# Sums of the output weights' quarters: from VectorE subtractions to DRAM copies and accumulating transfers

## The chip, the cores and the metric

The kernel runs on one core of a Trainium2 chip. The metric is the time of one execution in device microseconds. The engines are named as in the profile: PE (TensorE), PEld (its weight loads), DVE (VectorE), ACT (ScalarE), POOL (GpSimd) and SP (SyncE, which here only issues transfers). Sixteen DMA engines move the data.

## The reference

One encoder block with fp32 inputs: 1,024 tokens, width 2,048. A normalised input is projected to 5,632 columns; these feed windowed attention (16 heads, 4 key/value heads) and a bidirectional retention (8 heads); both branches are normalised and gated, put side by side and mixed by an output projection; residual and a final norm follow.

```python
h = rmsnorm(x, norm_w[l])
proj = jnp.einsum('bsd,de->bse', h, w_in[l])            # 1024 x 2048 x 5632
q_a, k_a, v_a, g_a, q_r, k_r, v_r, g_r = jnp.split(proj, points, axis=-1)
attn = rmsnorm(windowed_attention(q_a, k_a, v_a, ...), attn_out_norm_w[l]) * jax.nn.silu(g_a)
ret = head_groupnorm(bidirectional_retention(rotary(q_r), rotary(k_r) * 64**-0.5, v_r, ...), ret_gn_w[l]) * jax.nn.silu(g_r)
mixed = jnp.concatenate([attn, ret], axis=-1)
x = x + jnp.einsum('bse,ed->bsd', mixed, w_out[l])      # 1024 x 2048 x 2048
return rmsnorm(x, final_norm_w)
```

## The kernel before

**Arithmetic.** Every fp32 operand of the two projections is split into a rounded high part and the rest (`split`, L119 on): ACT casts the high part (`wh<-wr`, L127) and POOL or DVE subtracts it (`wl<-wr,wh`, L121). PE then makes three products per block: high by high, high by low, low by high.

**Input projection.** The weights come as 176 tiles of 128 x 512, called here by number from 0; 22 units (`UNITS`) of eight tiles each. `w_load` (L170) has SP load a tile into `wr` (two buffers), `w_split` (L175) makes `wh` and `wl` (two buffers each) of it. In the main loop (L919 on) each tile covers two steps of k; in the first of the two steps tile i + 1 is split and tile i + 2 loaded. The load's buffer is that of tile i, so SP waits until POOL has made `wl` of tile i. The buffers of `wh` and `wl` of tile i + 2 are free when PE has finished tile i.

**Work beside it.** After each quarter of a step `point` (L244) takes steps from three queues of generators: `jobs` (attention and retention), `aux` (evacuations, gates, the rotary step) and `slow` (bias rows, sums of weights, weighing and combining of rows). `slow` is served at two of three points, and at every point in the greater part of the output projection. The framework then orders each engine's instructions itself, so that work without dependences can stand well ahead of the place where it was issued.

**Output projection.** It works by a seven-product scheme on quarters, for each half f of the mixed width and each half u of the output columns: `quarter(f, u, j, q)` is the j-th tile of quarter q of the weights (q mod 2 is the column half, q // 2 the row half). Four of the seven products need a sum of quarters. These sums are made during the input projection by `w_combine` (L187): for each of the 16 (f, u, j) it loads the quarters into the two buffers `wc`, subtracts on DVE (L121), stores each sum into the DRAM tensor `wd`, and loads one of them again. A tile takes five loads, four subtractions and four stores. `w_src` (L163) later loads products 2 to 5 from `wd`. The same is done for the rows: `weigh_rows` scales the attention rows and `combine_rows` makes four combinations per (f, j) into the DRAM tensor `cd`, with three steps of `slow` between the loads and the DVE step. `done_with` (near the end) adds each finished product block into the output block e.

**Other parts the change touches.** `rope_post` loads the rotary tables just ahead of their use; in `attn_job` the gate of a block is loaded two steps ahead of the POOL multiplication that uses it.

Of the kernel before, what the change touches and what calls it, by code (L numbers as in the profile page):

```python
# [43 lines left out]
def hybrid_block(ctx: ExitStack, tc: tile.TileContext, a: dict, out: bass.AP):  # L44
# [57 lines left out]
    def wc_():  # L102
        return com.tile([128, 512], F32, tag="wc", name=nm("wc"), bufs=2)
# [82 lines left out]

    def w_combine(f):  # L187

        for u in range(2):
            for j in range(4):  # L190
                x, y = wc_(), wc_()
                SP.dma_start(x, quarter(f, u, j, 1))
                SP.dma_start(y, quarter(f, u, j, 0))
                yield from pause(3)
                tt(V, y, x, y, ALU.subtract)
                yield
                SP.dma_start(wd[f, u, 1, j], y)
                yield from pause(2)
                z = wc_()
                SP.dma_start(z, quarter(f, u, j, 3))  # L200
                yield from pause(3)
                tt(V, x, z, x, ALU.subtract)
                yield
                SP.dma_start(wd[f, u, 2, j], x)
                yield from pause(2)
                y = wc_()
                SP.dma_start(y, wd[f, u, 1, j])
                yield from pause(3)
                tt(V, z, z, y, ALU.subtract)
                yield  # L210
                SP.dma_start(wd[f, u, 0, j], z)
                v = wc_()
                SP.dma_start(v, quarter(f, u, j, 2))
                yield from pause(3)
                tt(V, v, v, z, ALU.subtract)
                yield
                SP.dma_start(wd[f, u, 3, j], v)
                yield from pause(2)

    def pause(n):  # L220
        for _ in range(n):
            yield
# [206 lines left out]
    def gate_post(tiles, et0, key):  # L429
# [7 lines left out]
        done.add(key)  # L437

    def rope_post(p, tiles, rq, rk):
        for hf in range(2):  # L440
            cs, sn = (retp[0].tile([128, 512], F32, tag="mr", name=nm("cs"), bufs=2) for _ in range(2))
            SP.dma_start(cs, a["cos"][:, 512 * hf : 512 * hf + 512])
            SP.dma_start(sn, a["sin"][:, 512 * hf : 512 * hf + 512])
            yield
            for et, dst in ((0, rq), (1, rk)):
                t = tiles[2 * et + hf]
                sh = retp[0].tile([128, 512], F32, tag="so", name=nm("sh"), bufs=2)
                V.stream_shuffle(sh, t, [i ^ 1 for i in range(32)])
                tt(V, t, t, cs, ALU.mult)
                yield  # L450
                tt(V, sh, sh, sn, ALU.mult)
                tt(V, dst[:, 512 * hf : 512 * hf + 512], t, sh, ALU.add)
                yield
        done.add(("rope", p))
# [4 lines left out]
    def attn_job(g, q_tiles, start):  # L459
# [36 lines left out]
        for t in range(32 + 8):  # L496
# [59 lines left out]
            if t >= 4 and t - 4 < 32:  # L556
# [220 lines left out]
    def weigh_rows():  # L777

        for hf in range(2):
            sl = slice(512 * hf, 512 * hf + 512)  # L780
            for kk in range(8):
# [3 lines left out]
                SP.dma_start(r, row)  # L785
                yield from pause(3)
                stt(V, r, r, ew[:, kk : kk + 1], n, ALU.mult, ALU.mult)
# [4 lines left out]
    def combine_rows(f, j, tile):  # L792

        if f:
            yield lambda: ("ret", j) in done
        for n, (x0, x1, op) in enumerate((
            (q_mix(f, j, 2), q_mix(f, j, 3), ALU.add),
            (q_mix(f, j, 0), q_mix(f, j, 2), ALU.subtract),
            (cd[f, 1, j], q_mix(f, j, 0), ALU.subtract),
            (q_mix(f, j, 1), cd[f, 0, j], ALU.subtract),  # L800
        )):
            x, y = tile(), tile()
            SP.dma_start(x, x0)
            SP.dma_start(y, x1)
            yield from pause(3)
            tt(V, y, x, y, op)
            yield
# [114 lines left out]
    for u, (kind, i) in enumerate(UNITS):  # L922
# [3 lines left out]
        for k in range(NK):  # L926
            step[0] = 16 * u + k
            wi, kk = divmod(step[0], 2)
            if kk == 0:
                w_split(wi + 1)  # L930
                w_load(wi + 2)
            if u == 0:
# [5 lines left out]
            for b in range(4):  # L938
# [16 lines left out]
                if last:  # L955
# [4 lines left out]
                    evac(u, b, p, st)  # L960
                point()
            if kind == "vr" and k == 9:
                if i == 0:
# [4 lines left out]
                else:  # L968
                    drain(jobs, ("ret", i - 1))
                raw = rope_t[i]  # L970
                rope_t[i] = (t4(), t4())
# [145 lines left out]
    for n in range(nprod):  # L1117
# [44 lines left out]
        def done_with(t):  # L1162
# [147 lines left out]
```

## Time and profile before

| what | value |
|---|---|
| median of three runs | 1634.11 us (1631.43 to 1637.33) |
| the profiled execution | 1634.68 us, its span 1632.9 us |
| mean TensorE clock granted | 0.976 of full |
| PE, PEld busy | 1530.8 us (94%), 1303.9 us (80%) |
| DVE, ACT, POOL busy | 890.5 us, 594.5 us, 467.3 us |
| moved by DMA | 261.49 MB, 160 GB/s in the mean |

The input projection takes the first 1,280 us or so, with attention beside it from about 200 us to 840 us and retention to 1,300 us; the output projection fills the rest. In a row of a timeline stand the start, the length (both in us), the engine, the line, the operation, out<-in, the shapes, and in brackets the idle time of the engine just before and what ended it. In a row of waits stand engine, line and tile that waited, what it waited for, and then the total in us, the number of times and the longest.

### The profile page before, as it was taken

The numbers are of one execution on the slowest core, as the hardware profiler recorded it, in microseconds if no ns is written. First come the engines' busy times: TensorE is split into PE (matmuls) and PEld (weight loads), VectorE is DVE, ScalarE is ACT, GpSimd is POOL, SyncE is SP. The second block draws the span as 40 slices with busy tenths as digits, with TensorE's granted clock in tenths as the row PEclk, the third lists the DMA queues.
The fourth block names the chain that finished last, engine by engine and source line by source line (L and its number), as shares of the span: only waits on it lengthen the run. The fifth ranks groups of instructions, "written<-read, shape, count | busy, mean of one in ns | idle before, by whom it ended". The sixth has DMA issues, their size and how long they took to land. (4 is left out here: it accounts for less than half of the span.)

```text
span 1632.9 us, 23154 instructions
## 1 busy us (share of the span) xinstructions
PE 1530.8 (94%) x8146; PEld 1303.9 (80%) x8146; DVE 890.5 (55%) x2000; ACT 594.5 (36%) x1254; POOL 467.3 (29%) x475
## 2 busy tenths in 40 slices
PE   8989998999999999999989989989989899899994
PEld 6977886778777887888988877888888777788883
DVE  5432265645665577566455655664647633537645
ACT  5321146543756367467411010110114322324434
POOL 2222222332343333334432221331323344420001
PEclk9999999999999999999999999999999999999998
DMA  8685545465445322312154554553255478666446
GB/s 294 244 240 170 174 150 163 163 196 163 152 148 178 106 62 72 84 57 79 49 162 149 171 190 149 181 187 101 82 180 168 136 235 274 213 217 195 124 122 226
DMA packets 163218, 261.49 MB, mean 160 GB/s; under 512 B 27371, under 2 KB 48875, under 8 KB 162972
## 3 DMA queue, kind: packets, MB, share of 16 engines
q1 hardware_dynamic: 163100, 259.99, 50.6%
q8 instruction: 64, 1.05, 0.3%
q14 instruction: 54, 0.44, 0.1%
HBM read 192.26 MB, written 67.67 MB: 159 GB/s over the span
## 5 line engine op out<-in xcount | busy, mean ns | idle before, releaser
L121 POOL TENSOR_TENSOR wl<-wr,wh 128x512 fp32r<-128x512 f32 x232 | 314.3, 1356 | 709.3 <-ACT wh L127 687.4
L127 ACT CAST wh<-wr 128x512 fp32r<-128x512 f32 x288 | 178.3, 619 | 608.0 <-PE psM L953 246.8
L121 DVE TENSOR_TENSOR wc<-wc,wc 128x512 f32<-128x512 f32 x92 | 79.5, 864 | 223.3 <-DMA wc<-in_w_out 98.2
L512 DVE CUSTOM_DVE_ANT_0 P<-psS,bias,nsink 128x384 f32<-128x384 f32 (+1 forms) x128 | 74.1, 579 | 60.5 <-PE psS L506 54.0
L516 ACT ACTIVATE P<-P,nmx 128x384 f32<-128x384 f32 (+1 forms) x128 | 75.6, 591 | 83.5 <-DVE nmx L512 82.3
L121 POOL TENSOR_TENSOR acc<-acc,sq 64x128 f32<-64x128 f32 x112 | 54.6, 487 | 170.3 <-ACT sq L545 159.1
L952 PE MATMUL psM<-h0r,wh 128*128 128x512 f32 x136 | 60.3, 445 | 31.7 <-DVE v L862 22.7
L121 DVE TENSOR_TENSOR PTl<-psT,PTh 128x384 fp32r<-128x384 f32 (+1 forms) x128 | 66.4, 519 | 26.7 <-ACT PTh L575 24.4
L121 DVE TENSOR_TENSOR wl<-wr,wh 128x512 fp32r<-128x512 f32 x56 | 38.6, 690 | 64.6 <-ACT wh L127 64.3
L564 PE MATMUL psT<-ident,P 128*128 128x128 f32 x352 | 61.2, 278 | 12.4 <-DVE PTl L121 12.1
L575 ACT CAST PTh<-psT 128x384 fp32r<-128x384 f32 (+1 forms) x128 | 57.7, 451 | 31.6 <-PE psT L564 29.5
L524 DVE TENSOR_SCALAR P<-P,sums 128x384 f32<-128x384 f32 (+1 forms) x128 | 60.2, 512 | 1.9
L952 PEld LDWEIGHTS psM<-h0r,wh 128*128 128x128 f32 x136 | 28.5, 210 | 40.5 <-issue 22.7
L564 PEld LDWEIGHTS psT<-ident,P 128*128 128x128 f32 x352 | 42.4, 141 | 22.1 <-DVE PTl L121 18.7
L953 PE MATMUL psM<-h0r,wh 128*128 128x512 f32 x136 | 57.8, 426 | 0.0
L954 PE MATMUL psM<-h0r,wl 128*128 128x512 f32 x136 | 56.9, 423 | 0.0
L952 PE MATMUL psM<-h7r,wh 128*128 128x512 f32 x136 | 56.0, 412 | 0.0
L537 PE MATMUL psO<-PTl,t 128*128 128x256 f32 x176 | 47.1, 296 | 9.1 <-DVE PTl L121 8.9
L952 PE MATMUL psM<-h4r,wh 128*128 128x512 f32 x136 | 55.5, 408 | 0.0
L952 PE MATMUL psM<-h5r,wh 128*128 128x512 f32 x136 | 55.5, 408 | 0.0
L952 PE MATMUL psM<-h6r,wh 128*128 128x512 f32 x136 | 55.1, 405 | 0.0
L952 PE MATMUL psM<-h3r,wh 128*128 128x512 f32 x136 | 55.0, 404 | 0.0
(508 smaller groups left out, 4660.8 us busy)
## 6 DMA issues: line engine op xcount, KB each, us to landing
wr<-in_w_in SPq DMA_DIRECT2D x176, 256.0 KB, 2.8
wc<-in_w_out SPq DMA_DIRECT2D x64, 256.0 KB, 2.9
wd<-wc SPq DMA_DIRECT2D x64, 256.0 KB, 2.0
wr<-wd SPq DMA_DIRECT2D x64, 256.0 KB, 2.7
wc<-md SPq DMA_DIRECT2D x62, 256.0 KB, 3.2
wr<-in_w_out SPq DMA_DIRECT2D x48, 256.0 KB, 2.8
t<-in_x SPq DMA_DIRECT2D x16, 512.0 KB, 5.7
gd<-t SPq DMA_DIRECT2D x32, 256.0 KB, 3.3
```

What stands on the lines that cost most here:

```text
L121: eng.tensor_tensor(o, x, y, op)
L127: A.copy(o_hi, x)
L512: V.tensor_tensor_reduce(x[:, :W], p[:, :W], bias[2 * pr + c][:, k0 : k0 + W], -1.0, nsink[:, head : head + 1], ALU.add, ALU.min, nmx[:, c ...
L516: A.activation(x[:, :W], x[:, :W], AF.Exp, bias=nmx[:, c : c + 1], scale=-1.0, accum_out=sums[:, c : c + 1])
L524: V.tensor_scalar(y[:, :W], y[:, :W], sums[:, cc : cc + 1], None, ALU.mult)
L537: T.matmul(o[:, :256], vs3[:, m0 + i, :], lo[:, i, :, :], start=False, stop=(i == m1 - m0 - 1))
L564: T.transpose(p[:, 128 * i : 128 * i + 128], x[:, 128 * i : 128 * i + 128], ident)
L575: A.copy(hi[:, :nk, c, :], p3)
L952: T.matmul(p, wh[:, ws], hh[:, sl], start=first, stop=False)
L953: T.matmul(p, wh[:, ws], hl[:, sl], start=False, stop=False)
L954: T.matmul(p, wl[:, ws], hh[:, sl], start=False, stop=last)
```

## The change

The 64 subtractions of `w_combine`, with their 80 loads and 64 stores, are gone. With quarters 1 and 2 taken with the other sign, all four sums become plain additions: q0 + q1, q1 + q3, q0 + q1 + q3 and the sum of all four (the first and last with turned sign as a whole). They are made in DRAM: SP issues 16 copies of 1 MiB from the weights into `wd` (four tiles of a quarter each), and POOL issues 64 transfers of 256 KB that add a quarter, or an earlier sum, to what is in `wd`. For the turned signs the row combinations are subtractions the other way round or of the negative, and `done_with` subtracts the product block where the output block's number is odd.

The waits between load and DVE step in the row work grow from three steps to eight; `slow` is served at every point from point 900 on; the load of a weight tile moves to the second of the tile's two steps; the gate of a block is loaded one step later; the rotary tables are loaded ahead of the step that uses them.

```diff
-    def w_combine(f):
-        for u in range(2):
-            for j in range(4):
-                x, y = wc_(), wc_()
-                SP.dma_start(x, quarter(f, u, j, 1))
-                SP.dma_start(y, quarter(f, u, j, 0))
-                yield from pause(3)
-                tt(V, y, x, y, ALU.subtract)
-                yield
-                SP.dma_start(wd[f, u, 1, j], y)
...
-                v = wc_()
-                SP.dma_start(v, quarter(f, u, j, 2))
-                yield from pause(3)
-                tt(V, v, v, z, ALU.subtract)
-                yield
-                SP.dma_start(wd[f, u, 3, j], v)
-                yield from pause(2)
+    def w_sums():
+        fu = [(f, u) for f in range(2) for u in range(2)]
+        for kind, q in ((1, 0), (2, 1), (0, 0), (3, 2)):
+            for f, u in fu:
+                i0 = 16 * (2 * u + q % 2) + 8 * f + q // 2
+                SP.dma_start(wd[f, u, kind], a["w_out"][i0 : i0 + 7 : 2])
+                yield from pause(4)
+        for kind, q in ((1, 1), (2, 3), (0, None), (3, None)):
+            for f, u in fu:
+                for j in range(4):
+                    src = wd[f, u, 2 if kind == 0 else 0, j] if q is None else quarter(f, u, j, q)
+                    G.dma_start(wd[f, u, kind, j], src, accum_op=ALU.add, max_dma_last_dim=2048)
+                    yield from pause(5)
...
-        if pt[0] % 3 or wide[0] is not None:
+        if pt[0] % 3 or pt[0] > 900:
             pump(slow, 1)
...
+    def rope_tabs(hf):
+        for name in ("cos", "sin"):
+            tabs[hf, name] = retp[0].tile([128, 512], F32, tag="mr", name=nm(name), bufs=2)
+            SP.dma_start(tabs[hf, name], a[name][:, 512 * hf : 512 * hf + 512])
...
                     PT[b] = tuple(
                         att.tile([128, 3, 2, 128], F32R, tag=w, name=nm(w), bufs=1) for w in ("PTh", "PTl")
                     )
+                else:
                     gt = att.tile([64, 2, 128], F32, tag="gt", name=nm("gt"), bufs=2)
...
-                yield from pause(3)
+                yield from pause(8)
                 stt(V, r, r, ew[:, kk : kk + 1], n, ALU.mult, ALU.mult)
...
-            (q_mix(f, j, 2), q_mix(f, j, 3), ALU.add),
-            (q_mix(f, j, 0), q_mix(f, j, 2), ALU.subtract),
-            (cd[f, 1, j], q_mix(f, j, 0), ALU.subtract),
-            (q_mix(f, j, 1), cd[f, 0, j], ALU.subtract),
+            (q_mix(f, j, 3), q_mix(f, j, 2)),
+            (q_mix(f, j, 0), q_mix(f, j, 2)),
+            (cd[f, 1, j], q_mix(f, j, 0)),
+            (q_mix(f, j, 1), cd[f, 0, j]),
...
-            yield from pause(3)
-            tt(V, y, x, y, op)
+            yield from pause(8)
+            if n < 2:
+                tt(V, y, x, y, ALU.subtract)
+            else:
+                stt(V, y, x, -1.0, y, ALU.mult, ALU.subtract)
...
-    slow.append((w_combine(0), None))
     slow.append((bias_copies(2), None))
     slow.append((bias_copies(3), None))
-    slow.append((w_combine(1), None))
+    slow.append((w_sums(), None))
...
             if kk == 0:
                 w_split(wi + 1)
+            else:
                 w_load(wi + 2)
...
+            if kind == "vr" and i and k == 5:
+                rope_tabs(0)
...
-            tt(V, d, banks[t], d, ALU.add)
+            tt(V, d, d, banks[t], ALU.subtract if e % 2 else ALU.add)
```

**Where the copies stand on SP.** In the changed program, between the loads of weight tiles 34 and 37 (`wr_1693` is tile 34, `wr_1863` tile 37); a wait for `DMAHWn` is for an earlier SP transfer, one for `Pool` for the POOL split of the tile two before. L194 is the copy into `wd`; the first of the 16 stands after the load of tile 17, the last is the last L194 row here.

```order
L194 DMA wd<-in_w_out 4x4x16384 [waits DMAHW6_49]
L172 DMA wr_1693<-in_w_in 128x512 [waits DMAHW7_49,Pool_49]
L194 DMA wd<-in_w_out 4x4x16384 [waits DMAHW0_49]
L172 DMA wr_1744<-in_w_in 128x512 [waits DMAHW1_49,Pool_49]
L194 DMA wd<-in_w_out 4x4x16384 [waits DMAHW2_49]
L172 DMA wr_1801<-in_w_in 128x512 [waits DMAHW7_49,DMAHW3_49,Pool_49]
L194 DMA wd<-in_w_out 4x4x16384 [waits DMAHW4_49]
L459 DMA bias_1853<-bd 128x384 [waits DMAHW5_49]
L172 DMA wr_1863<-in_w_in 128x512 [waits DMAHW6_49,DMAHW1_49,Pool_49]
```

Twelve of the copies stand between the loads of tiles 27 and 37, about one to a tile, the first four between those of tiles 17 and 24; 19 weight loads and 32 other SP transfers stand between the first and the last.

**Where the accumulating transfers stand on POOL.** In the changed program, at the splits of tiles 35, 36 and 37; a wait for `DMASWn` is for an earlier POOL transfer (always the eighth before), and `DMAHW4` is the last copy above.

```order
L121 TENSOR_TENSOR wl_1772<-wr_1744,wh_1771 128x512 [waits PE_49,DMAHW1_49,Activation_49,Pool_49]
L200 DMA wd<-wd 128x512 [waits DMASW6_49]
L200 DMA wd<-wd 128x512 [waits DMASW7_49]
L200 DMA wd<-wd 128x512 [waits DMAHW2_49,DMASW0_49]
L200 DMA wd<-wd 128x512 [waits DMASW1_49]
L121 TENSOR_TENSOR wl_1829<-wr_1801,wh_1828 128x512 [waits DMAHW3_49,PE_49,Activation_49]
L200 DMA wd<-wd 128x512 [waits DMASW2_49]
L200 DMA wd<-wd 128x512 [waits DMASW3_49]
L200 DMA wd<-wd 128x512 [waits DMAHW4_49,DMASW4_49]
L200 DMA wd<-wd 128x512 [waits DMASW5_49]
L200 DMA wd<-wd 128x512 [waits DMASW6_49]
L121 TENSOR_TENSOR wl_1897<-wr_1863,wh_1896 128x512 [waits DMAHW6_49,PE_49,Activation_49]
```

Before, these splits follow each other with nothing between them but two small attention steps. Now the 64 transfers, issued in the program over some sixty tiles, all stand between the splits of tiles 17 and 38, up to eight between two splits.

**The evacuation of the second `vr` unit on DVE.** `v<-psM` empties the banks that PE needs for the next unit, `wc` are row combinations. Before:

```order
L121 TENSOR_TENSOR wc_9422<-wc_9421,wc_9422 128x512 [waits DMAHW6_49,DMAHW7_49,DMAHW1_49,DVE_49]
L862 TENSOR_SCALAR v_9688<-psM_9121,rcol 128x256 [waits PE_49]
L862 TENSOR_SCALAR v_9688<-psM_9121,rcol 128x256
L121 TENSOR_TENSOR wc_9527<-wc_9526,wc_9527 128x512 [waits DMAHW3_49,DMAHW5_49,DMAHW2_49,DVE_49]
L862 TENSOR_SCALAR v_9706<-psM_9123,rcol 128x256 [waits PE_49]
L862 TENSOR_SCALAR v_9706<-psM_9123,rcol 128x256
```

And in the changed program:

```order
L124 SCALAR_TENSOR_TENSOR wc_9611<-wc_9610,wc_9611 128x512 [waits DMAHW1_49,DMAHW6_49,DMAHW0_49,DVE_49]
L858 TENSOR_SCALAR v_9452<-psM_8883,rcol 128x256 [waits PE_49]
L858 TENSOR_SCALAR v_9452<-psM_8883,rcol 128x256
L858 TENSOR_SCALAR v_9472<-psM_8885,rcol 128x256 [waits PE_49]
L858 TENSOR_SCALAR v_9472<-psM_8885,rcol 128x256
```

One combination no longer stands between the two evacuations; three still stand ahead of them, as before.

More of the change, by code (lines that the diff above doesn't have):

```diff
@@ L437, in gate_post @@
         done.add(key)
+    tabs = {}
+    def rope_tabs(hf):
+        for name in ("cos", "sin"):
+            tabs[hf, name] = retp[0].tile([128, 512], F32, tag="mr", name=nm(name), bufs=2)
+            SP.dma_start(tabs[hf, name], a[name][:, 512 * hf : 512 * hf + 512])
     def rope_post(p, tiles, rq, rk):
         for hf in range(2):
[L441 to L444, printed above, removed]
+            cs, sn = tabs.pop((hf, "cos")), tabs.pop((hf, "sin"))
             for et, dst in ((0, rq), (1, rk)):
@@ L452, in rope_post @@
                 tt(V, dst[:, 512 * hf : 512 * hf + 512], t, sh, ALU.add)
+                yield
+            if hf == 0:
+                rope_tabs(1)
+                yield
+                yield
                 yield
@@ L785, in weigh_rows @@
                 SP.dma_start(r, row)
-                yield from pause(3)
+                yield from pause(8)
                 stt(V, r, r, ew[:, kk : kk + 1], n, ALU.mult, ALU.mult)
@@ L795, in combine_rows @@
             yield lambda: ("ret", j) in done
-        for n, (x0, x1, op) in enumerate((
-            (q_mix(f, j, 2), q_mix(f, j, 3), ALU.add),
-            (q_mix(f, j, 0), q_mix(f, j, 2), ALU.subtract),
-            (cd[f, 1, j], q_mix(f, j, 0), ALU.subtract),
-            (q_mix(f, j, 1), cd[f, 0, j], ALU.subtract),
+        for n, (x0, x1) in enumerate((
+            (q_mix(f, j, 3), q_mix(f, j, 2)),
+            (q_mix(f, j, 0), q_mix(f, j, 2)),
+            (cd[f, 1, j], q_mix(f, j, 0)),
+            (q_mix(f, j, 1), cd[f, 0, j]),
         )):
@@ L969, in hybrid_block @@
                     drain(jobs, ("ret", i - 1))
+                if i == 0:
+                    rope_tabs(0)
                 raw = rope_t[i]
```

13 lines of the change are left out of this document (removed).

## The prediction

> **What bounds the kernel now.** I read the page's busy shares first, then busy time by stages (columns: busy us and number of instructions of PE, PEld, DVE, ACT, POOL; granted clock, DMA share, GB/s), then the waits.
>
> ```profile
> PE 1530.8 (94%) x8146; PEld 1303.9 (80%) x8146; DVE 890.5 (55%) x2000; ACT 594.5 (36%) x1254; POOL 467.3 (29%) x475
> 105.00:223.00 118.00, 115.33 (x524) 95.50 (x523) 35.21 (x63) 27.74 (x54) 27.26 (x22) 1.00 0.61 184
> 223.00:560.00 337.00, 320.32 (x1568) 265.77 (x1567) 191.32 (x470) 177.91 (x399) 111.45 (x134) 0.98 0.52 161
> ```
>
> PE bounds it: 1632.9 - 1530.8 = 102 us of the span are all that anything but fewer matmuls could win, and the change leaves the matmuls. From 105 to 223 us, where the copies and accumulating transfers will stand, PE idles 2.7 us; from 223 to 560 us, the rest of what `w_combine` covers, 16.7 us. The second thing to see is how the weight tiles flow there. POOL's timeline at the splits of tiles 16, 17, 18, 26, 27 and 37, SP's at the place where the first copy will be and at two loads, then from the waits (total us, times, longest) and the DMA issues (count, size, us to land) the rows that belong to it:
>
> ```profile
> 104.58 1.29 POOL L121 TENSOR_TENSOR wl<-wr,wh 128x512 fp32r<-128x512 f32 x1 [4.04 <-ACT wh L127]
> 112.21 1.29 POOL L121 TENSOR_TENSOR wl<-wr,wh 128x512 fp32r<-128x512 f32 x1 [6.34 <-ACT wh L127]
> 115.95 1.29 POOL L121 TENSOR_TENSOR wl<-wr,wh 128x512 fp32r<-128x512 f32 x1 [2.44 <-ACT wh L127]
> 160.78 1.29 POOL L121 TENSOR_TENSOR wl<-wr,wh 128x512 fp32r<-128x512 f32 x1 [5.46 <-ACT wh L127]
> 166.22 1.29 POOL L121 TENSOR_TENSOR wl<-wr,wh 128x512 fp32r<-128x512 f32 x1 [4.15 <-ACT wh L127]
> 222.54 1.30 POOL L121 TENSOR_TENSOR wl<-wr,wh 128x512 fp32r<-128x512 f32 x1 [4.42 <-ACT wh L127]
> 105.67 0.42 SPq L425 DMA_DIRECT2D kd<-t  x1
> 162.10 0.33 SPq L172 DMA_DIRECT2D wr<-in_w_in  x1
> 167.54 0.34 SPq L172 DMA_DIRECT2D wr<-in_w_in  x1
> SPq L172 <- POOL wl L121: 302.2, 152, 7.4
> ACT wh L127 <- DMA wr<-in_w_in: 11.5, 3, 8.3
> wr<-in_w_in SPq DMA_DIRECT2D x176, 256.0 KB, 2.8
> wd<-wc SPq DMA_DIRECT2D x64, 256.0 KB, 2.0
> ```
>
> A tile takes PE 5.44 us (160.78 to 166.22). A load goes out as soon as POOL has split the tile two before (160.78 + 1.29, load at 162.10) and lands after 2.8 us, at about 164.9; ACT needs it two tiles later, at 171.0 (171.66 less the cast's 0.6): 6 us in hand. The split ends about 3.4 us before PE begins the tile (5.44 less cast, split and gaps of 2). So POOL, SP and the transfers have near 10 us in hand, and lateness beyond that is PE's, tile by tile, because two buffers let nobody run further ahead.
>
> **The change part by part.**
>
> *Removed.* 144 SP transfers of 256 KB and 64 DVE steps.
>
> ```profile
> L121 DVE TENSOR_TENSOR wc<-wc,wc 128x512 f32<-128x512 f32 x92 | 79.5, 864 | 223.3 <-DMA wc<-in_w_out 98.2
> PE psT L564 <- DVE PTl L121: 12.1, 14, 1.9
> PE psO L537 <- DVE PTl L121: 8.9, 7, 3.6
> ```
>
> 64 x 0.864 = 55 us of DVE, and up to 98 us in which DVE stood waiting for a quarter. DVE is 55% busy, so most of it lies under PE. What reaches PE is its wait for attention's `PTl`, 21 us in all, of which 16.7 us is the whole idle time of 223 to 560 us. Bounds: 0 (attention's own chain) to 16.7; I take half, **-8**.
>
> *Added, the copies.* Each is 1 MiB in 4 pieces (4x4x16384) where the tiles of the trace have 128 rows. No row shows a DRAM-to-DRAM copy, nor a transfer known to use fewer than 16 engines. The engines' rate comes from the 1 us slices of the first 40 us, where they are nine tenths busy or more:
>
> ```profile
> DMA  0069999999999996787897379981499958999999
> GB/s 0 8 125 389 262 301 352 373 410 408 418 420 385 381 360 114 259 305 234 301 313 295 139 233 401 369 303 49 72 383 401 332 143 246 348 385 410 418 401 373
> q1 hardware_dynamic: 163100, 259.99, 50.6%
> ```
>
> 420 / 16 = 26.2 GB/s for one engine; over the whole span it is 259.99 MB / (0.506 x 16 x 1632.9 us) = 19.7 GB/s, mostly in rows of 2 KB. If the 4 pieces go whole to 4 engines, each carries 256 KB a copy: 10.0 us at the first rate, 13.3 at the second. If all 16 share it: 2.5 to 3.3 us. I take four engines, since a transfer dealt out by its outermost count has four parts to deal, and 10.0 us, since the pieces are long.
>
> The Trainium skill, page "DMA: Bandwidth & Descriptors", section "Rules for kernel authors", speaks against this copy: the slowest dimension sets how many engines serve a transfer, and an outermost count c below 16 confines it to at most c of them. By it the copies are at the four-engine end; without it they could be at either. No run here shows it so far. The same page's "Specifications" give about 27 GiB/s an engine, an estimate of 9.0 us a copy, and the sum below would be 16 us lower.
>
> *Added, the accumulating transfers.* 64 of 256 KB, on the same engines. An engine's share is 16 KB: 0.63 us if adding costs no more than copying, 1.25 if source and destination are both read at that rate. Nothing bounds it above; I take 0.94.
>
> *Where it meets the path.* POOL's order puts the transfers that need the last copy ahead of the split of tile 37, and the first copy stands just behind a `kd<-t`, at 106 us. So those four engines must do, between 106 us and the split of tile 37 (222.5 us before, 116.5 us later): 16 copies x 10.0 = 160; 19 weight loads x 0.63 = 12; 32 other SP transfers of 128 to 256 KB, 17; 60 accumulating transfers x 0.94 = 56. Sum 245, less 116.5 and the 10 in hand: **+119**. The weight loads are queued behind the copies on those engines, so PE should lose it bit by bit: little over the first four copies (two tiles each), then about 10 us a tile from tile 28 to 37. With both low prices 227 - 126.5 = 100; with 13.3 for a copy and 0.83 to 1.66 for the rest, 213 + 16 + 23 + 100 - 126.5 = 225. What POOL itself spends on an issue has no row; SP's take 0.33 to 0.45, and while POOL waits for copies even 1 us each is covered. If that cover goes, 47 of them stand between nine splits.
>
> *The row combinations.* In retention PE waits for the evacuation `v`, which stands behind a combination that waits for its rows:
>
> ```profile
> PE psM L952 <- DVE v L862: 22.7, 5, 5.9
> 972.81 0.98 DVE L121 TENSOR_TENSOR wc<-wc,wc 128x512 f32<-128x512 f32 x1 [5.85 <-DMA wc<-md]
> 973.71 0.86 DVE L862 TENSOR_SCALAR v<-psM,rcol 128x256 f32<-128x256 f32 x2
> 979.51 0.69 DVE L121 TENSOR_TENSOR wc<-wc,wc 128x512 f32<-128x512 f32 x1 [4.93 <-DMA wc<-cd]
> 980.12 0.87 DVE L862 TENSOR_SCALAR v<-psM,rcol 128x256 f32<-128x256 f32 x2
> ```
>
> Eight steps of lag ought to end this, but the order moves only the combination at 979.51 (and one in the fourth such unit) behind the evacuations; three remain ahead. Bounds 0 to -22.7; I take two waits of about 3, **-6**.
>
> *Costed at nothing.*
>
> ```profile
> gt<-gd SPq DMA_DIRECT2D x64, 64.0 KB, 2.4
> DVE t L121 <- DMA cs<-in_cos: 8.9, 4, 6.4
> ```
>
> The weight load half a tile later: SP waits for POOL there anyway (302.2 us, 152 times); without that cover 2.7 of the 6 us in hand. The gate a step later: 2.4 us to land, a step of about 3; where it is late, POOL's next split is, with 3.4 in hand. Tables ahead of the rotary step: DVE waits 8.9 us for them in all, off the path. The subtraction in place of the addition: same form. The wait on `slow`'s longer row work: DVE's order in the last stage hardly moves.
>
> Sum: 119 - 8 - 6 = +105. The profiled execution took 1634.68 us, 1.8 more than its span and 0.6 over the median of the runs; the span becomes 1738, the median **1739 us**.
>
> **The rivals.**
>
> *All 16 engines share a copy* (the other side). Then 40 + 12 + 17 + 38 = 107 us of engine time in 116.5: no stall, and the gains stand: 1634 - 14 = 1620. It decides from about 11 engines on (640/11 + 67 = 125, within the 126.5). For it: the 256 KB rows above land in 2.0 to 2.8 us, which one or four engines at 26.2 GB/s could not do, so 16 is what the trace knows. Against it: four pieces.
>
> *The same, but accumulating costs more*: 1.25 each, 40 + 12 + 17 + 75 = 144, 18 over what is covered: 1634 + 18 - 14 = 1638, no change that shows.
>
> *Accumulating is slower than two reads*: at 2.5 us each, 160 + 12 + 17 + 150 - 126.5 = 213, 1833 with the gains. From about 1.7 it is worth more than the doubts about a copy. For it: an addition is no copy, and no row prices it. Against: nothing but the bytes.
>
> *Weight loads pass the copies* instead of queueing. Then only POOL's wait counts: 160 + 2 to land less 116.5 and 3.4 gives 42, time 1634 + 42 - 14 = 1662. For it: the queue order inside an engine is not in the trace. Against: all SP transfers are one queue (q1).
>
> **How the numbers follow.** Forecast 0.60; slow accumulating 0.12; loads that pass 0.08; sixteen engines 0.15; sixteen with dear accumulating 0.05. 0.3% (4.9 us) is about what measurement can tell from no change. Faster is the sixteen-engine case, 0.15; the same is most of the dear one, 0.04; the rest is slower, 0.81. The forecast's own range is 1705 (100 and gains of 29) to 1855 (225, small gains). The range from 1630 to 1855 takes in all cases but the faster one and the tail of slow accumulating.
>
> **What would show it.** Right: PE's idle time between 106 us and tile 37 grows from 3 to over 100 us, with the DMA share low (four engines are 0.25) while ACT waits for `wr<-in_w_in` far above 11.5 us and POOL for DMA `wd`; splits ten or more us late each from tile 28. Then the 16.7 us of idle time of 223 to 560 halved, and the waits on `v` about 6 us lower. Wrong: tiles at 5.44 us through the stage with a DMA share near 1 in it (16 engines); or, with the stall, POOL waiting on its own transfers rather than on copies.

## The result and the profile after

The changed kernel takes 1761.2 us (median of four runs, 1759.5 to 1762.5), the kernel before 1632.8 in the same comparison: ratio 1.078, 95% interval 1.0756 to 1.0805. It is 128 us slower, where the prediction had +105.

The page of the profile after: busy times, the granted clock and the DMA share in 40 slices, the two DMA queues (packets, MB, share of 16 engines).

```profile
span 1757.8 us, 22916 instructions
...
PE 1559.3 (89%) x8146; PEld 1319.3 (75%) x8146; DVE 844.0 (48%) x1936; ACT 588.3 (33%) x1250; POOL 512.1 (29%) x539
...
PEclk9998966689999999999999999998999899999998
DMA  8767656573222232222223555545324567767346
...
q1 hardware_dynamic: 142684, 239.01, 42.8%
q0 software_dynamic: 9216, 16.78, 5.8%
```

The same 8,146 matmuls are counted on PE, but they take 28.5 us more (1559.3 against 1530.8), and PE's idle time goes from 102.1 to 198.5 us: 96.4 + 28.5 makes the 124.9 us between the spans. The clock shows where: slices 6 to 8, at 220 to 350 us, have 0.6. Busy time by stages (columns as in the prediction) shows it closer:

```profile
105.00:223.00 118.00, 85.83 (x356) 67.42 (x356) 4.45 (x8) 13.41 (x22) 35.10 (x36) 0.87 0.72 191
223.00:400.00 177.00, 97.96 (x346) 72.95 (x346) 34.76 (x97) 32.00 (x79) 52.70 (x60) 0.72 0.64 154
240.00:280.00 40.00, 4.79 (x17) 3.08 (x15) 0.00 (x0) 0.62 (x1) 3.25 (x4) 0.59 0.38 114
383.00:668.00 285.00, 283.68 (x1417) 238.44 (x1416) 132.41 (x354) 153.60 (x344) 100.59 (x127) 1.00 0.29 81
```

From 105 to 400 us PE stands for 111 us; from 240 to 280 it does next to nothing. From tile 38 on (383 us) it hardly waits any more. The waits of the whole run (total, times, longest) name what was late:

```profile
ACT wh L127 <- DMA wr<-in_w_in: 163.6, 18, 22.2
POOL wd L200 <- DMA wd<-in_w_out: 103.9, 15, 18.1
...
PE psM L948 <- ACT wh L127: 50.5, 9, 14.6
PE psM L950 <- POOL wl L121: 48.1, 8, 26.8
...
POOL wd L200 <- DMA wd<-wd: 27.9, 13, 10.9
...
PE psM L948 <- DVE v L858: 15.2, 3, 5.7
```

ACT's wait for weight tiles was 11.5 us before. POOL waits 132 us with an accumulating transfer (L200) for earlier transfers, and the splits (`wl`) are queued behind it. The name `wd<-in_w_out` stands both for the copies on SP and for the first 32 accumulating transfers on POOL itself. Up to 245 us POOL waits for copies (first row here, 105 to 245 us); after that it waits for its own transfers, the eighth before each time (second row, 245 to 400 us, and the 27.9 us on `wd<-wd` above). Those that it issued from 220 to 238 us took 49.4 us in the median to land (third row):

```profile
POOL wd L200 <- DMA wd<-in_w_out: 61.6, 7, 14.4
...
POOL wd L200 <- DMA wd<-in_w_out: 42.3, 8, 18.1
...
wd<-in_w_out POOLq DMA_DIRECT2D x7, 256.0 KB, 49.4
```

POOL's timeline around the worst place:

```profile
235.35 1.27 POOL L121 TENSOR_TENSOR wl<-wr,wh 128x512 fp32r<-128x512 f32 x1 [0.66 <-ACT wh L127]
236.56 0.81 POOL L200 DMA_DIRECT2D wd<-in_w_out  x1
255.50 0.81 POOL L200 DMA_DIRECT2D wd<-in_w_out  x1 [18.13 <-DMA wd<-in_w_out]
...
268.78 0.81 POOL L200 DMA_DIRECT2D wd<-in_w_out  x1 [10.48 <-DMA wd<-in_w_out]
277.78 0.81 POOL L200 DMA_DIRECT2D wd<-in_w_out  x1 [8.19 <-DMA wd<-in_w_out]
...
284.58 1.55 POOL L121 TENSOR_TENSOR wl<-wr,wh 128x512 fp32r<-128x512 f32 x1
...
379.85 1.58 POOL L121 TENSOR_TENSOR wl<-wr,wh 128x512 fp32r<-128x512 f32 x1
```

Between two splits (the first row and the `wl` row at 284.58) lie 49 us. The last row is the split of tile 37: 157 us later than before (222.54). The table gives these starts for the runs below, in us. Tiles are counted by their splits, and a row with `x2` is two of them.

| kernel | tile 37 | tile 80 | median us |
|---|---|---|---|
| before | 222.5 | 544.6 | 1633 |
| after | 379.9 | 668.1 | 1761 |
| e1 | 298.4 | 597.5 | 1689 |
| e2 | 314.6 | 602.8 | 1690 |
| e6 | 222.0 | 521.2 | 1611 |
| e10 | 294.0 | 581.4 | 1672 |
| e11 | 252.6 | 542.8 | 1633 |
| e12 | 317.9 | 605.0 | 1696 |

At tile 80 the distance between before and after is 123.5 us, at the end 125: on balance, the change's cost is there by then. The stretch from tile 38 to 80, which took 314.8 us before, is quicker by 30:

```profile
229.80:544.60 314.80, 298.12 (x1465) 247.19 (x1464) 176.89 (x443) 169.49 (x379) 105.56 (x128) 0.98 0.53 163
```

### The profile page after: what moved, and what is told of

It reads as the page before. It is cut to its first block, busy times and chain, and to the rows that moved or that the text cites. A ratio compares the mean times of both kernels' runs of the same rounds, so it can differ in the third digit from the quotient of the medians.

```text
span 1757.8 us, 22916 instructions
## 1 busy us (share of the span) xinstructions
PE 1559.3 (89%) x8146; PEld 1319.3 (75%) x8146; DVE 844.0 (48%) x1936; ACT 588.3 (33%) x1250; POOL 512.1 (29%) x539
## 3 DMA queue, kind: packets, MB, share of 16 engines
q8 instruction: 64, 1.05, 0.2%
## 4 chain that ended last, share of the span: by engine, by line
PE 56%; DMA 20%; DVE 10%; issue 5%; ACT 5%; POOL 3%; SPq 2%; POOLq 0%; ACTq 0%; DVEq 0%
PE psM L948 10%; PE psM L950 10%; PE psM L949 10%; DMA wd<-in_w_out 5%; DMA wc<-br 3%; PE psM L1179 2%; PE psM L1180 2%; PE psM L1178 2%; POOL wl L121 2%; DMA wd<-wd 2%; PE psM L942 2%; PE psM L943 2%; PE psM L941 2%; DMA wr<-in_w_out 2%; PE psT L556 2%
## 5 line engine op out<-in xcount | busy, mean ns | idle before, releaser
L121 DVE TENSOR_TENSOR t<-psM,rb 128x512 f32<-128x512 f32 x64 | 42.2, 686 | 216.3 <-PE psM L950 216.1
L948 PE MATMUL psM<-h0r,wh 128*128 128x512 f32 x136 | 58.6, 433 | 29.4 <-DVE v L858 15.2
L950 PE MATMUL psM<-h7r,wl 128*128 128x512 f32 x136 | 55.8, 410 | 26.8 <-POOL wl L121 26.8
L121 DVE TENSOR_TENSOR u<-psO,sq 64x256 f32<-64x256 f32 x64 | 26.6, 415 | 100.1 <-ACT sq L533 60.3
L948 PE MATMUL psM<-h2r,wh 128*128 128x512 f32 x136 | 56.8, 418 | 11.5 <-ACT wh L127 11.5
L950 PE MATMUL psM<-h4r,wl 128*128 128x512 f32 x136 | 54.9, 404 | 13.6 <-POOL wl L121 13.6
L950 PE MATMUL psM<-h1r,wl 128*128 128x512 f32 x136 | 54.3, 399 | 5.7 <-POOL wl L121 5.7
L200 POOL DMA_DIRECT2D wd<-in_w_out x32 | 27.2, 1133 | 102.5 <-DMA wd<-in_w_out 102.5
## 6 DMA issues: line engine op xcount, KB each, us to landing
wd<-wd POOLq DMA_DIRECT2D x32, 256.0 KB, 21.6
```

The costliest lines, as they stand in the source:

```text
L121: eng.tensor_tensor(o, x, y, op)
L948: T.matmul(p, wh[:, ws], hh[:, sl], start=first, stop=False)
L950: T.matmul(p, wl[:, ws], hh[:, sl], start=False, stop=last)
```

## The experiments

**e1: copies on 16 engines.** The copy is written so that its outermost count is 128 rows; nothing else is touched in the source.

```diff
-                SP.dma_start(wd[f, u, kind], a["w_out"][i0 : i0 + 7 : 2])
+                SP.dma_start(wd[f, u, kind].rearrange("j p c -> p j c"), a["w_out"][i0 : i0 + 7 : 2].rearrange("j p c -> p j c"))
```

> The changed kernel with one edit: each copy of 1 MiB into wd is issued with its 128 rows outermost, then the four tiles (128x4x512 in place of 4x4x16384). Same bytes, same number of copies and of accumulating transfers. Theory (four engines carry the copies, and everything behind them waits): the copies cost 16 x 2.7 = 43 us of all 16 engines in place of 156 us of four; with 64 accumulating transfers at 8 rows x 0.178 = 1.42 us (91 us), 16 weight loads and the other transfers (28 us) 162 us stand against the 87 us from tile 17 to 33 and 10 us in hand: some 65 us late there in place of 157, so the time falls by about 90, to 1670 us (1650 to 1700). Rival (the accumulating transfers and POOL's in-order waits for them cost it, however the copies are dealt): the time stays within 20 us of 1761.

1688.9 us, ratio 1.0326 (1.0298 to 1.0355): 72 us of the loss gone, 56 left. Its stage from 105 us, and POOL's wait, which here is for copies alone:

```profile
105.00:223.00 118.00, 87.00 (x346) 68.50 (x345) 4.45 (x8) 13.09 (x22) 48.98 (x53) 0.87 1.03 269
```

```profile
POOL wd L200 <- DMA wd<-in_w_out: 75.2, 13, 10.6
```

Now all 16 engines are full. The framework also ordered the work otherwise (the last accumulating transfer behind the split of tile 32, not 37, and attention's first matmuls elsewhere), so e1 is not the changed kernel with one number altered; e10 below is.

**e2: no accumulating transfers.** The line with `G.dma_start` is left out, so `wd` holds single quarters and the output is not the reference's. PE's rows stand in the changed kernel's order.

> The changed kernel without its 64 accumulating transfers: wd then holds single quarters, so the output projection multiplies other numbers than the reference; all else is as in the changed kernel, copies at their places. Theory: the four engines still have 156 us of copies, 13 of weight loads and 17 of the rest against 116.5 and 10 in hand, so tile 37 is some 60 us late in place of 157, and the time is about 1664 us (1645 to 1690); ACT waits for the weight loads, POOL for ACT alone. Rival (the loss is POOL waiting for transfers ahead of its splits, the loads pass the copies): no stall, 1761 - 157 = 1604 us.

1690.2 us, ratio 1.0347 (1.032 to 1.0374). The split of tile 37 is 92.1 us late where the expectation had about 60, and the time lies at the upper end of its range. The loads are late behind the copies, since ACT's waits for them are there without any accumulating transfer (the row below, from 105 to 400 us, where the kernel before has none); the rival of loads that pass falls. Against the changed kernel the accumulating transfers are worth 71 us.

```profile
ACT wh L127 <- DMA wr<-in_w_in: 103.7, 12, 19.4
```

The DMA packets in this trace show the four engines directly. A copy is 16 packets of 64 KB, about 2.4 us each, so 9.7 us for each of four engines, and of the 163 us in which any such packet is under way, exactly four are for 154.

**e4 and e5: the change in two halves.** e4 has every edit but the sums (it keeps `w_combine` at its old place, with additions for the turned signs). e5 is the kernel before with only `w_sums` and the signs.

```diff
     slow.append((bias_copies(1), None))
+    slow.append((w_combine(0), None))
     slow.append((bias_copies(2), None))
     slow.append((bias_copies(3), None))
-    slow.append((w_sums(), None))
+    slow.append((w_combine(1), None))
```

That is e4 against the changed kernel; e5 has the same lines the other way round, against the kernel before.

> The changed kernel with the sums of the quarters made again by loads, VectorE additions and stores as before (with the turned signs, in the old places of the queue): all edits but the copies and accumulating transfers. Theory (the 30 us by which the changed kernel is quicker from tile 38 to 80 come from the removed VectorE steps and their loads): that gain is gone, and the time is 1625 to 1645 us, as before. Rival (they come from the later weight load, gate load and tables): about 1605 us.

> The kernel before with the copies and accumulating transfers alone (and the turned signs): lag of three steps, the weight load, gate, tables and queue pace as before. Theory (the whole loss and the whole gain in the first half are these transfers'): 1634 + 157 - 30 = 1761 us, within 20 of the changed kernel. Rival (the other edits lose time that they were not charged with, in the last stage above all, where the changed kernel is 8 us slower): 1735 us or less.

e4: 1638.0 us, ratio 1.0023 (0.9997 to 1.0049). e5: 1755.3 us, ratio 1.0744 (1.0716 to 1.0771). The sums are the whole effect; the lag, the pace of `slow`, the tables, the gate and the later weight load together give nothing that shows.

**e6, e7, e8: kept where the program issues them.** In the changed kernel the framework moves the accumulating transfers from the places where the program issues them (with these copies, tiles 36 to 95) up to tiles 17 to 37. Here each copy is tied behind the last weight load on SP, each accumulating transfer behind the last split on POOL. e6 has e1's copies, one a tile (after the loads of tiles 24 to 36), then one accumulating transfer a tile (36 to 95). e8 has the copies three tiles apart (24 to 67, transfers 69 to 123). e7 is e8 with the changed kernel's 4x4x16384 copies.

```diff
-                SP.dma_start(wd[f, u, kind], a["w_out"][i0 : i0 + 7 : 2])
+                with tc.issue_after(tail['SP']):
+                    SP.dma_start(wd[f, u, kind].rearrange("j p c -> p j c"), a["w_out"][i0 : i0 + 7 : 2].rearrange("j p c -> p j c"))
                 yield from pause(4)
...
-                    G.dma_start(wd[f, u, kind, j], src, accum_op=ALU.add, max_dma_last_dim=2048)
+                    with tc.issue_after(tail['G']):
+                        G.dma_start(wd[f, u, kind, j], src, accum_op=ALU.add, max_dma_last_dim=2048)
```

`tail` holds the last weight load and the last split on POOL. e7 and e8 have `pause(15)` in place of `pause(4)`.

> As the changed kernel, but each copy goes out as 128 rows of 4 x 2 KB (16 engines), and copies and accumulating transfers are kept at the place where the program issues them: a copy behind the loads of tiles 24 to 36, about one a tile, and one accumulating transfer a tile behind the splits of tiles 36 to 95. Theory (what hurt is that the transfers are bunched ahead of tile 37, first on four engines, then with 48 accumulating transfers in ten tiles): an accumulating transfer takes some 1.5 us of each engine in a tile of 5.5 us and is hidden; the copies are 2.5 us each on top of a DMA share of 0.61, so 13 x 5.5 us of tiles hold 44 + 40 us of engine time, about 10 late, covered by the 10 in hand; the 15 us of PE idle time that w_combine cost before are gone: 1615 to 1630. Rival (the accumulating transfers themselves, by POOL's issue or by the loads queued behind them, cost PE about 1 us each wherever they stand): 1634 + 64 - 15 = 1683.

> As the changed kernel with the copies in four pieces as they are there (four engines), but kept where the program issues them and further apart: one copy for about three weight tiles (behind the loads of tiles 24 to 67), then one accumulating transfer a tile (tiles 69 to 123). Theory (a copy holds four engines for 10 us, and a weight load behind it is late by no more than the 10 us in hand if the next copy comes 16 us later): 1615 to 1640. Rival (each four-engine copy delays the load behind it by more than what is in hand, wherever it stands, as the 84 us for 16 copies without accumulating transfers suggest, 5 us each): 1634 + 84 - 15 = 1703.

> As e7, with the copies on 16 engines. Theory: nothing is late, all 15 us that w_combine cost PE are gained: 1612 to 1622. Rival (accumulating transfers cost about 1 us each wherever they stand): 1683. Second rival (PE has other waits in place of those on w_combine's DVE steps, or the row work that comes later in the same queue is late): 1630 or above.

e6: 1613.7 us, ratio 0.9874 (0.9855 to 0.9893), as the theory had it. It was run again:

> The kernel of e6 once more, for its interval and for a profile at the usual clock: 1609 to 1618 by either theory; PE idle between 105 and 223 us no more than 3 us and none of the 15 us that w_combine cost between tiles 38 and 80.

1610.5 us, ratio 0.9858 (0.9832 to 0.9884): faster than both kernels. All rows of e6 shown here, in the table too, are of this run. Its stages (the last is tile 38 to 80):

```profile
105.00:223.00 118.00, 116.97 (x535) 97.05 (x534) 20.93 (x46) 28.17 (x55) 28.06 (x23) 1.00 0.83 266
223.00:400.00 177.00, 176.79 (x889) 149.66 (x888) 89.68 (x246) 97.70 (x227) 77.85 (x97) 1.00 0.52 114
229.30:521.20 291.90, 290.47 (x1465) 244.48 (x1464) 147.12 (x400) 169.66 (x379) 135.85 (x174) 1.00 0.52 116
```

The sums cost PE nothing here. Tile 38 to 80 takes 291.9 us in place of 314.8 with the same number of PE rows: idle time 16.7 to 1.4, and 7.6 us less in the matmuls themselves, at a granted clock of 1.00 in place of 0.98. The accumulating transfers land in 4.3 to 4.4 us, a plain load in 2.8:

```profile
q0 software_dynamic: 9216, 16.78, 6.4%
...
wr<-in_w_in SPq DMA_DIRECT2D x176, 256.0 KB, 2.8
...
wd<-in_w_out POOLq DMA_DIRECT2D x32, 256.0 KB, 4.3
wd<-wd POOLq DMA_DIRECT2D x32, 256.0 KB, 4.4
```

e8: 1632.1 us, ratio 0.9988 (0.9969 to 1.0006): its second rival, not the theory. It stands level with e6 at tile 80 (520.3 us) and loses later, for instance here (e6, then e8):

```profile
824.00:884.00 60.00, 55.32 (x278) 46.23 (x279) 33.72 (x79) 5.92 (x10) 18.53 (x16) 0.94 0.51 165
```

```profile
824.00:884.00 60.00, 48.38 (x231) 39.72 (x232) 27.14 (x58) 5.78 (x11) 20.21 (x20) 0.89 0.60 163
```

Two things stand there that e6 has behind it or elsewhere: the last accumulating transfers, and row work that comes later because it follows the sums in the same queue. Which of the two costs the 20 us no run shows.

e7: 1724.0 us, ratio 1.0565 (1.054 to 1.0591), near the rival's 1703, and the theory fell. But the rival's reason did not hold either, as the next run showed.

**e9: is it the engines in e7?** The copies of e7 written with 16 pieces, so that 16 engines serve them:

```diff
-                    SP.dma_start(wd[f, u, kind], a["w_out"][i0 : i0 + 7 : 2])
+                    SP.dma_start(wd[f, u, kind].rearrange("j (q p) c -> q j (p c)", q=16), a["w_out"][i0 : i0 + 7 : 2].rearrange("j (q p) c -> q j (p c)", q=16))
```

The framework orders each engine's rows by a plan of its own. With 4x4x16384 and with 16x4x4096 it makes nearly the same plan; with 128x4x512 another, in which attention's matmuls stand between the weight tiles' and not in bursts. From PE's order in the changed kernel against e1's (+ is the changed kernel), where attention begins:

```
-L497 MATMUL psS_1752<-t_105_1676,qj_1723 128x256
-L498 MATMUL psS_1752<-t_106_1677,qj_1723 128x256
 L948 MATMUL psM_1664<-h1r,wh_1666 128x512
 L949 MATMUL psM_1664<-h1r,wh_1666 128x512
@@ -1015,4 +1011,61 @@
 L949 MATMUL psM_1665<-h1r,wh_1666 128x512
 L950 MATMUL psM_1665<-h1r,wl_1667 128x512
+L497 MATMUL psS_1728<-t_105_1676,qj_1723 128x256
+L497 MATMUL psS_1752<-t_105_1676,qj_1723 128x256
+L498 MATMUL psS_1728<-t_106_1677,qj_1723 128x256
```

> As e7 (copies held three tiles apart), each copy as 16x4x4096, so on 16 engines; the order of PE is that of e7 but for some 50 rows of attention, while e8's, with 128x4x512, differs from it in some 400. Theory (four engines): as e8, 1625 to 1640. Rival (the order): as e7, 1700 to 1725.

1718.3 us, ratio 1.0526 (1.05 to 1.0552): as e7. So in e7 four engines cost some 6 us, and what parts e9 from e8 some 86: the order, and with it the size of the copies' pieces. Busy time from 230 to 250 us, e9 and then e8, and POOL's timeline there in e9:

```profile
230.00:250.00 20.00, 16.21 (x74) 12.09 (x73) 13.84 (x46) 12.11 (x37) 2.87 (x5) 0.82 0.05 14
```

```profile
230.00:250.00 20.00, 20.00 (x106) 17.22 (x105) 12.25 (x36) 11.55 (x29) 4.80 (x6) 1.00 0.36 110
```

```profile
234.71 0.46 POOL L121 TENSOR_TENSOR acc<-sq 64x128 f32<-64x128 f32 x1 [9.95 <-ACT sq L539]
...
240.76 0.45 POOL L121 TENSOR_TENSOR acc<-sq 64x128 f32<-64x128 f32 x1 [4.89 <-ACT sq L539]
...
249.43 2.54 POOL L121 TENSOR_TENSOR wl<-wr,wh 128x512 fp32r<-128x512 f32 x2 [7.53 <-issue]
```

In this stretch the DMA engines are idle (0.05) while PE waits, so what is late here is the order and not the copies: the weight tiles' splits stand on POOL behind attention's `acc`, which waits for a chain through PE, DVE and ACT, and then two splits come at once.

**e10: the same question for the changed kernel.** Only the copy's form differs, 16x4x4096 as in e9; every engine's rows stand in the changed kernel's order, row for row.

> The changed kernel with each copy written as 16x4x4096 (16 pieces of 4 x 16 KB) in place of 4x4x16384; every engine's instructions stand in the same order as in the changed kernel, row for row, so the number of engines that serve a copy is all that differs. Theory (what counts is that four engines carry the copies): 2.5 us a copy in place of 10, the time falls to that of e1, 1670 to 1700. Rival (the framework's planner takes a copy in few long pieces for slow and orders attention in bursts ahead of the weight tiles' splits; that fixed order costs the time, as PE's idle time at a DMA share of 0.05 in e7 suggests, and it is the same here): 1735 to 1765.

1672.2 us, ratio 1.0236 (1.021 to 1.0262). In the changed kernel four engines cost 89 us; the rival (order alone) falls here. A copy is now 64 packets of 16 KB, about 0.63 us each. From 105 us on the engines are full, with copies and accumulating transfers together:

```profile
105.00:223.00 118.00, 97.67 (x413) 78.64 (x412) 4.45 (x8) 14.71 (x24) 51.24 (x54) 0.90 1.01 268
```

**e11 and e12: the rest, taken apart.** Both are e6 with the copy in another form: 16x4x4096 (e11) and 4x4x16384 (e12). PE's rows stand in the changed kernel's order in both, and no row of any engine but the copy itself differs between the two.

> As e6 (copies and accumulating transfers kept at the program's place, 16 engines), but the copies written as 16x4x4096: with this form the planner puts PE's rows in the changed kernel's order, row for row, with attention's first matmuls in a burst, where e6 has them between the weight tiles. Theory (that order in itself costs little here; bunched accumulating transfers and four engines are what cost): 1612 to 1630. Rival (the order costs as it did in e9): 1645 to 1700.

> As e11 with copies of 4x4x16384 (four engines); every engine's rows in e11's order. Against e11 it prices four engines with no accumulating transfer near; against the changed kernel it prices the bunching of the accumulating transfers. Theory (16 copies of 10 us pass those four engines beside the weight loads in the 13 tiles after tile 24, as in e2, which lost 84 us by tile 37): 1680 to 1705. Rival (the accumulating transfers' bunch is not what costs the other 70 us between e2 and the changed kernel; their work costs PE wherever it stands): 1740 or above.

e11: 1633.2 us, ratio 0.9995 (0.9974 to 1.0015), between the two: the order costs 20 to 23 us against e6. The lateness comes in one step: at the split of tile 33 (the second in the first row here) e11 is within 2 us of e6, and tile 34 is split 38.5 us later, where e6 takes 4.8. Between them attention's burst stands, with POOL's splits behind its `acc` as in e9:

```profile
198.43 2.72 POOL L121 TENSOR_TENSOR wl<-wr,wh 128x512 fp32r<-128x512 f32 x2 [10.17 <-ACT wh L127]
221.02 0.45 POOL L121 TENSOR_TENSOR acc<-sq 64x128 f32<-64x128 f32 x1 [19.87 <-ACT sq L539]
...
238.19 2.70 POOL L121 TENSOR_TENSOR wl<-wr,wh 128x512 fp32r<-128x512 f32 x2 [11.77 <-ACT wh L127]
```

e12: 1696.3 us, ratio 1.0385 (1.0344 to 1.0425), as the theory had it. Their stages from 105 us, e11 and then e12:

```profile
105.00:223.00 118.00, 111.78 (x507) 89.92 (x505) 23.41 (x61) 29.84 (x65) 22.92 (x19) 1.00 0.75 248
223.00:400.00 177.00, 171.18 (x812) 142.36 (x812) 73.46 (x193) 79.78 (x183) 75.71 (x91) 0.95 0.51 117
```

```profile
105.00:223.00 118.00, 94.86 (x392) 74.92 (x391) 4.45 (x8) 13.94 (x23) 19.01 (x15) 0.88 0.49 169
223.00:400.00 177.00, 145.17 (x632) 115.17 (x631) 66.67 (x190) 70.49 (x167) 50.63 (x59) 0.87 0.42 122
```

Step by step from e6 to the changed kernel: 1611 to 1614 (e6); +20 to 23 for the order that goes with copies in long pieces (e11); +63 for four engines (e12); +65 for the accumulating transfers in a bunch and the first copies earlier (after). Without four engines that last step is 39 (e11 to e10). Between e1 and e6, whose copies have the same form and whose matmuls stand in the same order but for a few, it is 78. Whether the bunch costs this by full engines or by POOL's waits ahead of the splits, no run separates. e12 and e2 differ by 6 us, within their intervals: spread out, the accumulating transfers cost next to nothing.

## Why the prediction was right, and where its terms were off

**The copies on four engines: right.** Without accumulating transfers the prediction's sum is 160 + 12 + 17 - 126.5 = 62.5; e12 against e11 measures 63.1. That the two lie so close is in part luck. From the split of tile 16 to that of tile 80 (rows below) e12 takes 61.5 us more than e11, and 43 of them are idle time of PE; the other 18.5 are longer matmuls, for which the prediction had no term. That loads queue behind copies is e2's and e12's wait on ACT, 103.7 and 103.6 us. The 10.0 us taken for a copy were some 9.7 (e2). The Trainium skill, page "DMA: Bandwidth & Descriptors", section "Rules for kernel authors", was weighed there: an outermost count below 16 confines a transfer to at most that many engines. The runs agree, 89 us between e10 and the changed kernel with the same order.

The rows are the kernel before, the changed kernel, e2, e11 and e12, each from the split of tile 16 to that of tile 80:

```profile
104.58:544.63 440.05, 420.69 (x2025) 348.89 (x2024) 216.34 (x517) 200.53 (x442) 135.25 (x152) 0.99 0.55 169
104.88:668.09 563.21, 450.68 (x2040) 364.80 (x2040) 168.46 (x454) 195.05 (x438) 182.83 (x216) 0.88 0.48 125
105.73:602.79 497.06, 446.05 (x2040) 362.42 (x2039) 167.50 (x454) 195.35 (x438) 130.49 (x152) 0.93 0.33 108
104.10:542.81 438.71, 425.45 (x2040) 351.85 (x2040) 169.22 (x454) 195.10 (x438) 167.17 (x200) 0.98 0.57 150
104.75:605.00 500.25, 443.95 (x2040) 360.91 (x2039) 167.44 (x454) 195.49 (x438) 166.92 (x199) 0.93 0.48 132
```

**The accumulating transfers: about right on the path, under-priced on the engines.** The term was 60 x 0.94 = 56. Between e2 and the changed kernel tile 37 moves by 65.2 us and PE's idle time in the rows above by 61.5, so 1.0 to 1.1 us for each of the 60. That is what one costs PE, POOL's issues and waits included, and not what it takes of the engines. Queue q0's share on the page gives 0.058 x 1757.8 / 64 = 1.59 us of all 16 engines for one; by the same measure 256 KB of the plain queue q1 took 0.83 us before (0.506 x 1632.9 us for 259.99 MB). So the price lies beyond the upper bound of 1.25 and does not reach the 1.7 from which the rival of slow accumulating was to count; that the cost on the path came out near the term is luck. The Trainium skill, page "Collectives: The Full Stack", section "The bandwidth ceiling: the fold count and why AG ≠ RS ≠ AR", says of ReduceScatter, a collective that adds in the DMA engines, that the add makes it slower by its two source reads. The factor of 1.9 between 1.59 and 0.83 fits two reads in place of one; no run here shows the reads themselves.

**The order: missing.** The prediction took the order of the changed kernel as given, and read from it only where copies and transfers stand. That attention's first matmuls come in a burst there was in it too. Against e6, e11, with that order and 16 engines, is 30.5 us late at tile 37, 21.6 at tile 80 and 20 to 23 at the end. Part of the lateness at tile 37 is attention's work done early, which comes back: from there to tile 80 e11 has 1,441 matmuls and e6 1,500. So the 157 us of the changed kernel at tile 37 are not all loss, and are not what the forecast's 119 is to be set against.

**The matmuls' own time: missing.** From tile 16 to tile 80 the changed kernel takes 123 us longer than the kernel before. Of these 93 are idle time of PE (112.5 against 19.4) and 30 are time in matmuls, at a mean granted clock of 0.88 in place of 0.99. There are 15 more of them in the stretch, an estimate of 3 us at 0.19 us each; the rest is that they took longer, and over the whole run, with the same matmuls, it is 28.5 us. No term had it, and it is the largest that the sum lacked.

**The end of `w_combine`: -8 forecast, -23 measured**, outside its bound of -16.7. The bound was PE's idle time in the stretch, and that is indeed gone (e6: 15.3 us). The other 7.6 are shorter matmuls, at a granted clock of 1.00 in place of 0.98. In the changed kernel the stretch of tile 38 to 80 gives 30 us; there it has 1,417 PE rows in place of 1,465, so part of this is attention that was done during the stall.

**The row combinations: right in the wait, not in the time.** PE's wait on `v` fell from 22.7 to 15.2 us, 7.5 against the 6 forecast; e5, without the longer lag, has 19.9. In e4, with it, the wait on `v` is 17.6, but a wait of 5.3 on the evacuation `t` of the same line stands beside it, and e4 is no faster: 1.0023. Four other edits stand in e4, and no run takes them apart.

**The sum.** The forecast of +105 was 119 - 8 - 6. By PE's time the spans differ by 108.5 us of idle time up to tile 37 (111.2 against 2.7), -15.4 of idle time from there to tile 80 (1.3 against 16.7), 30 of time in matmuls up to there, and 1.4 after tile 80, where the forecast had its -6: 125 in all. So the stall was taken 10 too long and the gain of `w_combine` in idle time 7 too small, the -6 did not come, and the longer matmuls had no term. The errors cancel in part, and that the forecast came within 23 us of the 128 is owed to that.

**The signs named ahead.** Idle time of PE over 100 us: yes, 111. ACT on `wr<-in_w_in`: yes, 163.6. Idle time after tile 38 halved: more, nearly gone. A low DMA share, about 0.25: no, 0.72 and 0.64. Four busy engines are 0.25 alone, but the accumulating transfers ran beside the copies on all of them; without them (e2) it is 0.50 and 0.30, and 0.38 in the worst 40 us of the changed kernel. By that sign alone the four engines would have been ruled out wrongly. Splits ten or more us late each from tile 28: no. Of the 121 us lost from tile 27 to tile 37, 44 fall between tiles 30 and 31, where POOL waits for its own transfers, and 37 between tiles 33 and 34, where attention's burst stands. POOL waiting on its own transfers rather than on copies was named as a sign against the forecast, and it came half true: 61.6 us are for copies, 70.2 for its own. It does not overturn the four engines: in e10, with the same order, the two rows of L200 are 30.8 and 8.4 us in place of 103.9 and 27.9.

**The rivals.** Sixteen engines (1620) named the kernel that e6 is, 1611 to 1614, but only with the transfers spread; on sixteen engines alone, with everything else as in the change, it is 1672 (e10), 34 over the dear variant's 1638. There the same bunch fills all engines at a share of 1.01. The argument for this rival, that four engines could not land 256 KB in 2.0 to 2.8 us, holds for the 2.0 us alone: four shares of 64 KB at 26.2 GB/s are 2.5 us.

## What to carry to other kernels

Write a DRAM-to-DRAM copy so that its outermost count is at least the number of engines (16 and 128 here); four long pieces held four engines for 10 us a copy, and the loads on the same queue waited. Work without dependences is hoisted by the framework: tie it behind an instruction of its own engine, so that it spreads over the stretch that has DMA share to spare, and look at what else the new order moved, since a changed transfer form alone reordered attention here, at a cost of 20 to 23 us (e11) and some 86 (e9). A stall has a second price beside its idle time, in the clock.

## What the runs showed of the hardware

A copy written 4x4x16384 ran on four DMA engines, 16 packets of 64 KB at about 2.4 us each (e2); written 16x4x4096 it was 64 packets of 16 KB at about 0.63 us (e10). An accumulating transfer of 256 KB took 1.59 to 1.61 us of the 16 engines by its queue's share (e6: 0.064 x 1610.3 / 64), where 256 KB of plain traffic took 0.83 in the kernel before, and landed in 4.3 us where a plain load landed in 2.8. POOL spent 0.81 us on one issue. The granted clock was low where PE idled: 0.59 in the 40 us in which PE worked 4.8, 0.72 over 223 to 400 us. The same 8,146 matmuls took 28.5 us longer in the changed kernel, so the stall cost more than its idle time.
